# A transformer layer on one core: one engine's order kept in W_down, mixer weights stored by half, transposes in another PSUM bank

## The chip, the cores and the metric

The kernel runs on 1 core of one Trainium2 chip. The metric is the time of one execution on the device in microseconds (us), and the median of 3 runs counts. TensorE (PE) does the matrix products, VectorE (DVE), ScalarE (ACT) and GpSimd (POOL) the rest; SyncE (SP) issues most transfers.

## The reference

One decoder layer over 1024 tokens of width 1024, in float32:

```
h = RMSNorm_pre(x);  P = h @ W_in            # split into u, v, z, xbc, dt
A = u * (causal W_s v + b)                   # gated mixing in chunks of 128, 8 heads
B = Mamba-2 SSD(conv(xbc), dt) * silu(z)     # chunked scan, gated group norm
x = x + RMSNorm_post(concat[A, B] @ W_out)
f = relu(RMSNorm_pre2(x) @ W_up)^2           # 1024 -> 4096
x = x + RMSNorm_post2(f @ W_down)            # 4096 -> 1024
```

## The kernel before, in words

Every float32 product is made of three matmuls. An operand is split into a high part (a cast by ACT into a format that PE takes at full speed) and a low part (the operand less its high part, by DVE or POOL); `mm3` multiplies high by high, high by low and low by high. Names ending in `h` are high parts, those in `l` low ones; `wh` and `wl` are those of a mixer weight unit of 128 x 1024.

The mixer works on two halves of 512 tokens, H0 and then H1. Each half runs over units of `W_in`: the convolved blocks (`psB`, `psC`, `psx`), the state-space groups, then z, v and u (`psu`), then the output projection in units of `W_out` (`pso`). Between them stand a group norm (`psgr` out of `rr`) and the spatial mixing (`pssp`). `units` lists the weight units in the order of use; 28 of them are used by both halves. At first use `load_unit` loads the raw unit into `ws` (2 buffers), splits it, and `keep` stores both parts into DRAM (`wd`); at second use `again` loads both parts. While H0's u is made, `x1_tile` normalizes the four token tiles of the second half and transposes them on PE (`tx`) into `hT`; while H1's u is made, `h2_tile` transposes the MLP's input (`tf`) in the same way. A transposition fills two PSUM banks a tile; ACT takes the high part out (`hTh`), then DVE the low part (`hTl`). PSUM has 4 general banks (`mm_bank`), 2 for the state space (`ss_bank`) and 2 more (`mi_bank`); `psu` and `pso` lie in general ones.

W_up and W_down use a Strassen scheme with seven products for eight. In W_down `seq` lists pieces in super groups; the numbers 1, 5, 6, 3, 7, 2, 4 are the order of the products in one. A piece is 24 matmuls out of `f` (activations read back from DRAM, split by ACT and POOL) and `whd`, `wld` (a weight block `wr`, or a difference of blocks `wt` that DVE makes, split by ACT and DVE). The loop issues `preps[m + 2]` and then the matmuls of piece m; when a product is complete, `flush` adds its PSUM bank `pd` to an accumulator (`acc`): ACT copies the first time, DVE adds later. Two `pd` banks take turns, so PE can begin a new product only when the bank's last one has been flushed. A last group of plain products (`pl`) and the final norm follow.

The order of each engine's instructions is set by a scheduler that plays the program on a simulated timeline, except where `Engine.held` is true: each instruction of that engine is then tied behind the one that the program issued before it. Before, that holds in W_up for PE (`pe.held`), and at the tail for DVE. All instructions issued through `Engine` carry line 73 in the profile, so that they are told apart by their names.

Of the kernel before, what the change touches and what calls it, by code (L numbers as in the profile page):

```python
# [8 lines left out]
F32 = mybir.dt.float32  # L9
F32R = mybir.dt.float32r  # L10
# [5 lines left out]
P = 128  # L16
SEQ = 1024
D = 1024
# [16 lines left out]
N_SPLIT = 5  # L35
# [21 lines left out]
def hymba_kernel(ctx, tc, x, norm_mix_pre, w_in, gm_ln_w, gm_ln_b, gm_w_s, gm_b_s,  # L57
                 conv_w, conv_b, dt_bias, a_log, d_skip, ssm_norm_w, w_out,
                 norm_mix_post, norm_ffn_pre, w_up, w_down, norm_ffn_post, out):
    nc = tc.nc  # L60
# [21 lines left out]
    pe, act, dve, pool = [Engine(e) for e in (nc.tensor, nc.scalar, nc.vector, nc.gpsimd)]  # L82

    def pool_of(stack, name, **k):
        return stack.enter_context(tc.tile_pool(name=name, bufs=1, reuse_waits="tile", **k))
# [5 lines left out]
    wpool = pool_of(ctx, "wpool")  # L91
# [9 lines left out]
    dram = ctx.enter_context(tc.tile_pool(name="dram", bufs=1, space=bass.MemoryType.DRAM))  # L101
# [10 lines left out]
    def f(ap):  # L112
        return ap.bitcast(F32)
# [5 lines left out]
    def split_psum(h, l, src):  # L119
        act.copy(h, src)  # L120
        dve.tensor_tensor(l, src, f(h), op=ALU.subtract)
# [14 lines left out]
    def rstd_steps(ss, n, base=None):  # L136
        nsmall[0] += 1
        i = nsmall[0]
        w = ss.shape[-1]
        v = const.tile([P, w], F32, tag=f"rv{w}", bufs=2 if w == 1 else 1, name=f"rv{i}")  # L140
        r = const.tile([P, w], F32, tag=f"rr{w}", bufs=4 if w == 1 else 1, name=f"rr{i}")
        t = const.tile([P, w], F32, tag=f"rt{w}", bufs=2 if w == 1 else 1, name=f"rt{i}")
        ti = const.tile([P, w], I32, tag=f"rti{w}", bufs=2 if w == 1 else 1, name=f"rti{i}")
        yield r
        if base is None:
            dve.tensor_scalar(v, ss, 0.5 / n, 0.5 * EPS, op0=ALU.mult, op1=ALU.add)
        else:
            dve.tensor_scalar(v, ss, 0.5 / n, base, op0=ALU.mult, op1=ALU.add)
        yield
        dve.tensor_scalar(ti, v.bitcast(I32), 1, None, op0=ALU.logical_shift_right)  # L150
        yield
        dve.tensor_scalar(r.bitcast(I32), ti, -1.0, RSQRT_SEED, op0=ALU.mult, op1=ALU.add)
        for _ in range(3):
            yield
            if w == 1:
                dve.tensor_scalar(t, r, r, v, op0=ALU.mult, op1=ALU.mult)
            else:
                dve.tensor_mul(t, v, r)
                dve.tensor_mul(t, t, r)
            yield  # L160
            if w == 1:
                dve.tensor_scalar(r, t, 1.5, r, op0=ALU.subtract, op1=ALU.mult)
            else:
                dve.scalar_tensor_tensor(r, t, 1.5, r, op0=ALU.subtract, op1=ALU.mult)

    def row_rstd(ss, n, base=None):
        steps = rstd_steps(ss, n, base)
        r = next(steps)
        for _ in steps:
            pass  # L170
        return r
# [24 lines left out]
    units = xbu + zvu + wou[0:4] + xbu[0:4] + wou[4:8] + xbu[4:8] + zvu + wou  # L196
# [3 lines left out]
    ready = []  # L200
    loads = []
# [5 lines left out]
    staged = {}  # L207

    def stage_unit(i):
        kind, src = units[i]  # L210
        shape = [P, 8, P] if kind == "m" else [P, 2, 512]
        st = stage.tile(shape, F32, tag="ws", bufs=N_STAGE, name=f"ws{i}")
        loads.append(nc.sync.dma_start(st, src).ins.name)
        staged[i] = st, shape

    first, parts = {}, {}

    def load_unit(eng=None):
        i = state["load"]
        if i >= len(units):  # L220
            return
        state["load"] += 1
        if id(units[i]) in first:
            again(i)
            return
        first[id(units[i])] = i
        if i not in staged:
            stage_unit(i)
        st, shape = staged.pop(i)
        wh = wpool.tile(shape, F32R, tag="wh", bufs=N_SPLIT, name=f"wh{i}")  # L230
        wl = wpool.tile(shape, F32R, tag="wl", bufs=N_SPLIT, name=f"wl{i}")
        split(wh, wl, st, eng)
        ready.append((wh, wl))
        keep(i)

    def keep(i):

        if any(u is units[i] for u in units[i + 1:]):
            parts[i] = [dram.tile([P, 1024], F32, name=f"wd{i}{j}") for j in range(2)]
            for d, t_ in zip(parts[i], ready[i]):  # L240
                nc.sync.dma_start(d, f(t_.rearrange("p a b -> p (a b)")))

    def again(i):
        shape = [P, 8, P] if units[i][0] == "m" else [P, 2, 512]
        hl = [wpool.tile(shape, F32R, tag=t_, bufs=N_SPLIT, name=f"{t_}{i}") for t_ in ("wh", "wl")]
        for d, t_ in zip(parts[first[id(units[i])]], hl):
            ins = nc.sync.dma_start(f(t_.rearrange("p a b -> p (a b)")), d)
        loads.append(ins.ins.name)
        ready.append(tuple(hl))

    def next_unit(ahead=2, eng=None):
        i = state["use"]
# [6 lines left out]
    def norm_w(src, name, unit=None):  # L259
        w = now["nwp"].tile([P, D], F32, tag="nw", bufs=2, name=name)  # L260
        d = nc.sync.dma_start(w, src[0].partition_broadcast(P))
        if unit is not None:
            after(d, unit)
        return w

    def load_tok(src, name, unit=None):
        t = now["tok"].tile([P, D], F32, tag="tok", bufs=4, name=name)
        d = nc.sync.dma_start(t, src)
        if unit is not None:
            after(d, unit)  # L270
        return t

    x0 = {}
    for what in PRO_LOADS:
        if what == "w":
            wpre = norm_w(norm_mix_pre, "wpre")
        elif what in "ab":
            stage_unit("ab".index(what))
        else:
            t = int(what)  # L280
# [14 lines left out]
    def sumsq(src, name, ss=None):  # L295
        if ss is None:
            ss = const.tile([P, 1], F32, tag="ss", bufs=8, name=name)
        junk = now["tok"].tile([P, src.shape[-1]], BF16, tag="junk", bufs=1, name=f"{name}j")
        act.activation(junk, src, AF.Square, accum_out=ss)
        return ss  # L300

    def norm_transpose(xx, r, w, hT, t, name, bank):
        dve.scalar_tensor_tensor(xx, xx, r, w, op0=ALU.mult, op1=ALU.mult)
        transpose_split(xx, hT, t, name, bank)

    def transpose_split(xx, hT, t, name, bank):
        for q in range(2):
            ps = bank(f"{name}_{q}")
            pv = ps.rearrange("p (k c) -> p k c", c=P)
            for k in range(4):  # L310
                pe.transpose(pv[:, k, :], xx[:, (4 * q + k) * P:(4 * q + k + 1) * P], ident)
            split_psum(hT[0][:, 4 * q:4 * q + 4, t * P:(t + 1) * P],
                       hT[1][:, 4 * q:4 * q + 4, t * P:(t + 1) * P], pv)

    hT_tag = "hTh", "hTl"
    hT = tuple(hpool.tile([P, KB, HALF], F32R, tag=t_, bufs=1, name=t_) for t_ in hT_tag)

    def x1_tile(t):
        xx = load_tok(x[0, HALF + t * P:HALF + (t + 1) * P, :], f"x1_{t}", X1_AFTER + t)
        norm_transpose(xx, row_rstd(sumsq(xx, f"ssx1{t}"), D), wpre, hT, t, f"tx1{t}", mm_bank)  # L320

    mctx = stack()
    mpool = pool_of(mctx, "mpool")
# [477 lines left out]
    H0.v = tok_dense_gelu(H0, "v", dense_tok)  # L801
    v_norm(H0)
    H0.u = tok_dense_gelu(H0, "u", dense_tok_outer, lambda t: t and x1_tile(t - 1))
    x1_tile(3)
    wpost = norm_w(norm_mix_post, "wpost", X1_AFTER)
    wfpre = norm_w(norm_ffn_pre, "wfpre", X1_AFTER)
# [33 lines left out]

    def h2_tile(t):
        xx = load_tok(h2d[t * P:(t + 1) * P, :], f"h2r{t}")
        transpose_split(xx, hT, t, f"tf{t}", mm_bank)

    H1.u = tok_dense_gelu(H1, "u", dense_tok_outer, lambda t: t and h2_tile(t - 1))
    h2_tile(3)
    spatial(H1)
    sctx.close()
# [229 lines left out]
    for p in range(N_PAIR):  # L1078
        ahead = prep(p + 1)
        a = A[p]  # L1080
# [61 lines left out]
    def rows(g, h):  # L1142
        n, gi = sg_of[g]
        return raw_tile(2 * n + h)[:, 4 * gi:4 * gi + 4, :].rearrange("p (r c) n -> p r c n", r=2)

    def w_load(n, h, gs=None):
        for g in gs or SG[n]:
            for r in range(2):
                d = nc.sync.dma_start(rows(g, h)[:, r], downs[4 * g + 2 * r + h][1])
                wr_loads.append(d.ins.name)  # L1150
# [63 lines left out]
    def flush(i, ps):  # L1214
# [3 lines left out]
        else:  # L1218
            act.copy(a_, ps)
            done.add(INTO[i])  # L1220

    w_load(0, 0)
    floads[0]()
    w_load(0, 1)
# [147 lines left out]
```

## Time and profile before

| | us |
|---|---|
| median of 3 runs (1070.23 to 1070.66) | 1070.66 |
| profiled execution | 1074.9 |
| its span | 1073.1 |
| PE busy in it | 1023.7 |
| DVE, ACT, POOL busy | 743.8, 468.6, 313.3 |
| mean granted TensorE clock | 0.984 of full speed |

The stages, in us from the span's start: H0's mixer to about 172, H0's output projection and H1's mixer to 427, W_up to 741, W_down to 1020, the plain group to 1061, the last norm to the end. A busy share says little of a single stage; waits and windows do. In a timeline the bracket tells how long the engine was idle just before and on which instruction it waited.

### The profile page before, as it was taken

What the parts mean: (1) busy time and instruction counts of PE and PEld (TensorE: products, weight loads), DVE (VectorE), ACT (ScalarE), POOL (GpSimd) and SP (SyncE); (2) the same over time, 40 slices, a digit from 0 to 9 for tenths busy, and PEclk for the clock granted to TensorE, in tenths of its full rate; (3) what the DMA queues carried; (4) which work ended last, traced back from release to release, by engine and by line L of the source; (5) the groups of instructions that cost most, each with busy time, mean ns of one, the idle gap of its engine ahead of it and who ended that gap; (6) DMA issues with size and microseconds to landing.
All of it is one profiled execution on the core that took longest, in us unless ns stands there. A gap on an engine that the chain in (4) does not pass through costs nothing. (4 is left out here: it accounts for less than half of the span.)

```text
span 1073.1 us, 13234 instructions
## 1 busy us (share of the span) xinstructions
PE 1023.7 (95%) x4735; PEld 836.4 (78%) x4735; DVE 743.8 (69%) x1265; ACT 468.6 (44%) x642; POOL 313.3 (29%) x169
## 2 busy tenths in 40 slices
PE   5989998999999999999999999999699999999996
PEld 4777776777788888888788888787588888888885
DVE  5647978366954835677477777775976777776677
ACT  5547443244343423675444444445533333333421
POOL 4454332030001002400111111112734444444533
PEclk9999898999999999999999999999989999999998
DMA  8997745475974263766756677766842552443422
GB/s 267 313 320 279 259 172 196 137 247 185 389 269 165 97 223 121 229 195 200 249 194 219 230 235 235 228 215 238 309 157 98 177 177 84 145 152 136 145 84 98
DMA packets 138857, 216.46 MB, mean 202 GB/s; under 512 B 9652, under 2 KB 72232, under 8 KB 138792
## 3 DMA queue, kind: packets, MB, share of 16 engines
q1 hardware_dynamic: 104360, 196.74, 53.1%
q10 hardware_dynamic: 34432, 18.88, 6.0%
q8 instruction: 37, 0.61, 0.2%
q14 instruction: 28, 0.23, 0.1%
HBM read 143.73 MB, written 71.86 MB: 201 GB/s over the span
## 5 line engine op out<-in xcount | busy, mean ns | idle before, releaser
L73 PE MATMUL pd<-whd,f 128*128 128x512 f32 x752 | 234.2, 392 | 7.9 <-DVE acc L73 7.9
L73 PEld LDWEIGHTS pd<-whd,f 128*128 128x128 f32 x752 | 142.3, 189 | 38.2 <-DVE acc L73 8.4
L73 POOL TENSOR_TENSOR f<-fr,f 128x1024 fp32r<-128x1024 f32 x47 | 118.5, 2524 | 147.2 <-ACT f L73 147.2
L73 PE MATMUL pd<-wld,f 128*128 128x512 f32 x376 | 147.4, 392 | 0.8 <-DVE wld L73 0.8
L73 POOL TENSOR_TENSOR wl<-ws,wh 128x1024 fp32r<-128x1024 f32 x36 | 87.7, 2440 | 191.9 <-ACT wh L73 191.7
L73 ACT CAST f<-fr 128x1024 fp32r<-128x1024 f32 x47 | 49.4, 1053 | 146.2 <-issue 132.2
L73 POOL TENSOR_TENSOR wlb<-sa,whb 128x1024 fp32r<-128x1024 f32 x16 | 38.5, 2407 | 225.1 <-ACT whb L73 213.9
L73 PEld LDWEIGHTS pd<-wld,f 128*128 128x128 f32 x376 | 71.3, 190 | 16.1 <-DVE wld L73 1.2
L73 DVE TENSOR_TENSOR wld<-wt,whd 128x1024 fp32r<-128x1024 f32 x28 | 63.5, 2267 | 26.9 <-ACT whd L73 26.9
L73 ACT ACTIVATE u<-u 128x512 f32<-128x512 f32 (+1 forms) x66 | 44.3, 672 | 61.6 <-DVE u L73 55.7
L73 ACT CAST wh<-ws 128x1024 fp32r<-128x1024 f32 x44 | 46.1, 1049 | 53.1 <-DMA ws<-in_w_in_dram 17.5
L73 DVE TENSOR_TENSOR acc<-pd,acc 128x2048 f32<-128x2048 f32 x24 | 54.9, 2287 | 14.8 <-PE pd L73 14.8
L73 DVE TENSOR_TENSOR wld<-wr,whd 128x1024 fp32r<-128x1024 f32 x21 | 47.8, 2276 | 22.8 <-ACT whd L73 22.8
L73 ACT ACT_TABLE_LOAD x30 | 38.5, 1283 | 27.9 <-DVE gg L73 8.7
L73 PE MATMUL pe<-hTh,wh 128*128 128x512 f32 x128 | 50.3, 393 | 0.0
L73 PE MATMUL pe<-hTh,wl 128*128 128x512 f32 x128 | 49.9, 390 | 0.0
L73 PE MATMUL pe<-hTl,wh 128*128 128x512 f32 x128 | 49.9, 390 | 0.0
L73 DVE TENSOR_TENSOR u<-puB,s 128x512 f32<-128x512 f32 x32 | 22.1, 692 | 31.6 <-DMA s<-early 15.8
L73 DVE TENSOR_SCALAR gg<-gg,acs 128x128 f32<-128x128 f32 x64 | 21.4, 396 | 19.9 <-DMA gg<-acd 19.9
L73 PE MATMUL pso<-wh,mixbh 128*128 128x512 f32 x64 | 28.0, 438 | 6.6 <-DVE hTl L73 5.3
L73 DVE TENSOR_TENSOR wlc<-sa,whc 128x1024 fp32r<-128x1024 f32 x16 | 29.2, 1824 | 5.6 <-ACT whc L73 5.6
L73 ACT CAST whd<-wt 128x1024 fp32r<-128x1024 f32 x28 | 29.3, 1046 | 5.7 <-DVE wt L73 2.8
(342 smaller groups left out, 2652.2 us busy)
## 6 DMA issues: line engine op xcount, KB each, us to landing
fr<-fsp SPq DMA_DIRECT2D x49, 512.0 KB, 3.8
wu<-in_w_up_dram ACTq DMA_DIRECT2D x32, 512.0 KB, 5.1
wr<-in_w_down_dram SPq DMA_DIRECT2D x32, 512.0 KB, 5.5
wd<-wh SPq DMA_DIRECT2D x28, 512.0 KB, 4.0
wd<-wl SPq DMA_DIRECT2D x28, 512.0 KB, 5.2
wh<-wd SPq DMA_DIRECT2D x28, 512.0 KB, 4.6
wl<-wd SPq DMA_DIRECT2D x28, 512.0 KB, 4.2
fsp<-c SPq DMA_DIRECT2D x42, 256.0 KB, 2.1
```

The costliest lines, as they stand in the source:

```text
L73: ins = fn(*a, **k)
```

## The change

Three edits. First, `dve.held = True` stands before W_down's loop and no longer only before the tail, so that DVE works in the order in which the loop issues: low parts and differences for piece m + 2, then the flush of piece m. Second, `keep` stores only `wl`; `again` loads the raw weight once more from the input into a `ws` buffer, makes `wh` with an ACT cast, and loads `wl` from DRAM. Third, `x1_tile` and `h2_tile` transpose into the two `ss_bank` banks and not into the general ones.

```diff
@@ keep, again
         if any(u is units[i] for u in units[i + 1:]):
-            parts[i] = [dram.tile([P, 1024], F32, name=f"wd{i}{j}") for j in range(2)]
-            for d, t_ in zip(parts[i], ready[i]):
-                nc.sync.dma_start(d, f(t_.rearrange("p a b -> p (a b)")))
+            parts[i] = dram.tile([P, 1024], F32, name=f"wd{i}")
+            nc.sync.dma_start(parts[i], f(ready[i][1].rearrange("p a b -> p (a b)")))
 
     def again(i):
-        shape = [P, 8, P] if units[i][0] == "m" else [P, 2, 512]
-        hl = [wpool.tile(shape, F32R, tag=t_, bufs=N_SPLIT, name=f"{t_}{i}") for t_ in ("wh", "wl")]
-        for d, t_ in zip(parts[first[id(units[i])]], hl):
-            ins = nc.sync.dma_start(f(t_.rearrange("p a b -> p (a b)")), d)
-        loads.append(ins.ins.name)
-        ready.append(tuple(hl))
+        if i not in staged:
+            stage_unit(i)
+        st, shape = staged.pop(i)
+        wh, wl = [wpool.tile(shape, F32R, tag=t_, bufs=N_SPLIT, name=f"{t_}{i}") for t_ in ("wh", "wl")]
+        nc.sync.dma_start(f(wl.rearrange("p a b -> p (a b)")), parts[first[id(units[i])]])
+        act.copy(wh, st)
+        ready.append((wh, wl))
@@ x1_tile
-        norm_transpose(xx, row_rstd(sumsq(xx, f"ssx1{t}"), D), wpre, hT, t, f"tx1{t}", mm_bank)
+        norm_transpose(xx, row_rstd(sumsq(xx, f"ssx1{t}"), D), wpre, hT, t, f"tx1{t}", ss_bank)
@@ h2_tile
-        transpose_split(xx, hT, t, f"tf{t}", mm_bank)
+        transpose_split(xx, hT, t, f"tf{t}", ss_bank)
@@ before W_down's loop
+    dve.held = True
     w_load(0, 0)
```

The scheduler makes new orders of these. On DVE at W_down's start, before: the number in `wld_3` or `pd_5` is that of the product (product 3 goes on in the bank of product 5, `acc_6525` is the accumulator that it is added to), and the last number tells instances apart.

```order
L73 TENSOR_TENSOR wld_3_6608<-wr_6533,whd_3_6607 128x1024
L73 TENSOR_TENSOR wt_0_6566<-wr_6533,wt_0_6566 128x1024
L73 TENSOR_TENSOR wld_7_6644<-wt_0_6645,whd_7_6643 128x1024
L73 TENSOR_TENSOR wt_2_6866<-wr_6596 128x1024
L73 TENSOR_TENSOR wld_2_6681<-wr_6533,whd_2_6680 128x1024
L73 TENSOR_TENSOR wld_4_6716<-wt_0_6566,whd_4_6715 128x1024
L73 TENSOR_TENSOR wt_1_6908<-wr_6781,wt_1_6829 128x1024
L73 TENSOR_TENSOR wld_1_6752<-wr_6596,whd_1_6751 128x1024
L73 TENSOR_TENSOR wt_2_6945<-wr_6781,wt_2_6866 128x1024
L73 TENSOR_TENSOR acc_6525<-pd_5_6611,acc_6525 128x2048
```

The same place in the change:

```order
L73 TENSOR_TENSOR wld_3_6608<-wr_6533,whd_3_6607 128x1024
L73 TENSOR_TENSOR wt_0_6645<-wr_6533,wr_6528 128x1024
L73 TENSOR_TENSOR wld_7_6644<-wt_0_6645,whd_7_6643 128x1024
L73 TENSOR_TENSOR wld_2_6681<-wr_6533,whd_2_6680 128x1024
L73 TENSOR_TENSOR acc_6525<-pd_5_6611,acc_6525 128x2048
L73 TENSOR_TENSOR wt_0_6566<-wr_6533,wt_0_6566 128x1024
L73 TENSOR_TENSOR wld_4_6716<-wt_0_6566,whd_4_6715 128x1024
L73 TENSOR_TENSOR acc_6527<-pd_1_6570,acc_6527 128x2048
```

The first DVE `acc` moved up: it now stands right behind the low part for product 2, and the instructions for product 4 and for the next super group come after it.

On PE, at the end of H0's last `psu`, before: `tx` are the transposes of the second half's tiles 2 and 3, `pso_00` the first bank of the output projection.

```order
L73 MATMUL psu_1663<-wh_1511,hTl 128x512
L73 MATMUL tx_0_1708<-ident,x_2_1689 128x128 x4
L73 MATMUL tx_1_1715<-ident,x_2_1689 128x128 x4
L73 MATMUL tx_0_1742<-ident,x_3_1723 128x128 x4
L73 MATMUL tx_1_1749<-ident,x_3_1723 128x128 x4
L73 MATMUL pso_00_1816<-wh_1822,mixbh_1225 128x512
L73 MATMUL pso_00_1816<-wl_1823,mixbh_1225 128x512
```

In the change:

```order
L73 MATMUL psu_1623<-wh_1473,hTl 128x512
L73 MATMUL pso_00_1776<-wh_1782,mixbh_1197 128x512
L73 MATMUL pso_00_1776<-wl_1783,mixbh_1197 128x512
L73 MATMUL pso_00_1776<-wh_1782,mixbl_1198 128x512
L73 MATMUL pso_00_1776<-wh_1782,mixbh_1197 128x512
L73 MATMUL pso_00_1776<-wl_1783,mixbh_1197 128x512
L73 MATMUL pso_00_1776<-wh_1782,mixbl_1198 128x512
L73 MATMUL pso_01_1777<-wh_1782,mixbh_1197 128x512
L73 MATMUL pso_01_1777<-wl_1783,mixbh_1197 128x512
L73 MATMUL tx_0_1668<-ident,x_2_1649 128x128 x4
```

The output projection moved ahead of the transposes; those of tile 3 now stand behind `psgr`.

On PE at the program's start, before: `psB` and `psC` are the first two convolved blocks of H0.

```order
L73 MATMUL psB_0_296<-hTh,wh_148 128x256
L73 MATMUL psC_0_430<-hTh,wh_232 128x256
L73 MATMUL psC_0_430<-hTl,wh_232 128x256
L73 MATMUL psB_0_296<-hTl,wh_148 128x256
L73 MATMUL psB_0_296<-hTh,wl_149 128x256
```

In the change:

```order
L73 MATMUL psB_0_290<-hTh,wh_148 128x256
L73 MATMUL psC_0_422<-hTh,wh_230 128x256
L73 MATMUL psC_0_422<-hTl,wh_230 128x256
L73 MATMUL psx_0_486<-hTh,wh_284 128x256
L73 MATMUL psx_0_486<-hTl,wh_284 128x256
L73 MATMUL psB_0_290<-hTl,wh_148 128x256
L73 MATMUL psB_0_290<-hTh,wl_149 128x256
```

Two matmuls of the third block, `psx`, moved up among those of the first two.

## Rows read from the trace of the kernel before

**Rows 1.** The page's busy times by engine, with share and instructions.

```profile
PE 1023.7 (95%) x4735; PEld 836.4 (78%) x4735; DVE 743.8 (69%) x1265; ACT 468.6 (44%) x642; POOL 313.3 (29%) x169
```

**Rows 2.** Windows (PE, PEld, DVE, ACT, POOL busy; clock; DMA share; GB/s), full stretches.

```profile
300.00:400.00 100.00, 100.00 (x513) 82.70 (x512) 55.99 (x140) 35.53 (x49) 8.10 (x9) 1.00 0.50 177
...
500.00:600.00 100.00, 99.42 (x435) 81.09 (x434) 63.34 (x87) 46.71 (x66) 16.86 (x7) 1.00 0.68 222
...
800.00:900.00 100.00, 100.00 (x443) 82.84 (x442) 76.21 (x39) 36.09 (x36) 43.77 (x19) 1.00 0.42 139
```

**Rows 3.** Waits of PE (total us, times, longest us).

```profile
PE pd L73 <- DVE acc L73: 7.9, 1, 7.9
PE pso L73 <- DVE hTl L73: 5.3, 2, 4.0
PE psC L73 <- DVE gg L73: 3.3, 1, 3.3
...
PE psgr L73 <- DVE rr L73: 2.7, 1, 2.7
```

**Rows 4.** Windows around the two largest waits.

```profile
170.00:180.00 10.00, 6.05 (x34) 5.00 (x33) 10.00 (x11) 6.33 (x8) 7.08 (x3) 0.96 0.89 308
180.00:190.00 10.00, 8.69 (x33) 6.60 (x31) 4.11 (x13) 0.00 (x0) 0.73 (x1) 0.69 0.66 236
...
775.00:780.00 5.00, 2.15 (x5) 1.76 (x6) 5.00 (x4) 0.00 (x0) 2.81 (x1) 0.50 0.51 150
780.00:785.00 5.00, 5.00 (x16) 3.92 (x16) 3.49 (x3) 0.00 (x0) 0.00 (x0) 0.65 0.18 64
```

**Rows 5.** Timeline of DVE at W_down's start (start us, us, instruction).

```profile
758.83 1.21 DVE L73 TENSOR_TENSOR wld<-wt,whd 128x1024 fp32r<-128x1024 f32 x1
...
762.23 3.42 DVE L73 TENSOR_TENSOR wld<-wt,whd 128x1024 fp32r<-128x1024 f32 x1
...
775.52 2.28 DVE L73 TENSOR_TENSOR acc<-pd,acc 128x2048 f32<-128x2048 f32 x1
```

**Rows 6.** Timeline of POOL in the same stretch.

```profile
761.07 16.74 POOL L73 TENSOR_TENSOR f<-fr,f 128x1024 fp32r<-128x1024 f32 x5 [4.39 <-ACT f L73]
```

**Rows 7.** DVE's groups in W_down, 800 to 900 (busy us, mean ns, idle before).

```profile
L73 DVE TENSOR_TENSOR wld<-wt,whd 128x1024 fp32r<-128x1024 f32 x11 | 26.5, 2406 | 9.2 <-ACT whd L73 9.2
...
L73 DVE TENSOR_TENSOR wld<-wr,whd 128x1024 fp32r<-128x1024 f32 x8 | 18.6, 2325 | 11.4 <-ACT whd L73 11.4
```

**Rows 8.** Timeline of PE at H0's output projection.

```profile
172.81 1.91 PE L73 MATMUL tx<-ident,x 128*128 128x128 f32 x16
178.66 0.50 PE L73 MATMUL pso<-wh,mixbh 128*128 128x512 f32 x1 [3.95 <-DVE hTl L73]
...
182.39 0.80 PE L73 MATMUL pso<-wh,mixbh 128*128 128x512 f32 x1 [1.31 <-DVE hTl L73]
...
188.37 1.05 PE L73 MATMUL psgr<-ident,rr 128*128 128x128 f32 x8
```

**Rows 9.** Timeline of DVE there.

```profile
177.93 0.68 DVE L73 TENSOR_TENSOR hTl<-tx,hTh 128x512 fp32r<-128x512 f32 x1
...
183.59 0.15 DVE L73 SCALAR_TENSOR_TENSOR rr<-rt,rr 128x4 f32<-128x4 f32 x1
```

**Rows 10.** Timeline of ACT at the program's start.

```profile
22.22 1.05 ACT L73 CAST wh<-ws 128x1024 fp32r<-128x1024 f32 x1 [4.75 <-DMA ws<-in_w_in_dram]
```

**Rows 11.** Timeline of PE at the program's start.

```profile
19.67 0.28 PE L73 MATMUL psB<-hTh,wl 128*128 128x256 f32 x1
19.79 0.28 PE L73 MATMUL psB<-hTh,wh 128*128 128x256 f32 x1
...
24.38 1.86 PE L73 MATMUL tx<-ident,x 128*128 128x128 f32 x15 [1.21 <-ACT x L73]
```

**Rows 12.** DMA issues: packets' size, median us to landing.

```profile
wh<-wd SPq DMA_DIRECT2D x28, 512.0 KB, 4.6
...
ws<-in_w_in_dram SPq DMA_DIRECT2D x20, 512.0 KB, 6.6
```

## Prediction

> **What bounds the kernel now.** I read the page's busy shares first. TensorE (PE) works 1023.7 us of a span of 1073.1 us and no other engine more than 743.8 [rows 1], so time can be gained only where PE stands idle or runs at its lower clock, some 49 us in all, and it is lost wherever an edit makes PE wait. Windows along the span come next: the reader should see that PE is full between 300 and 400, almost full in W_up between 500 and 600, and full in W_down's middle between 800 and 900 [rows 2]. So a change of ours must be judged in the remaining stretches. The waits of PE name them [rows 3]: 7.9 us once in W_down, for VectorE (DVE) to add a finished PSUM bank to an accumulator (`acc`), 5.3 us in two waits for DVE's `hTl` at the start of the first half's output projection, 3.3 us for `gg` and 2.7 us for `rr` in the mixer. The clock in windows comes last: after the two largest waits the granted TensorE clock is 0.69, 0.50 and 0.65 of full speed [rows 4], so that part of the time PE is at the lower of its two levels, 1.2 GHz. A wait is thus dearer than its idle time. The order of each engine's program, of before and of the change, says what stands ahead of the waited-for instructions.
>
> All sums stand against the profiled execution, which took 1074.9 us (span 1073.1); the median of the runs is 1070.66, 4.2 us less, and I take the change to be the same in both.
>
> **Edit 1, W_down's DVE order: -9 us.** In 100 us of steady W_down PE runs 443 matmuls [rows 2], 0.226 us each; a piece of 24 is 5.4 us. PE resumes when `acc` ends, at 775.52 + 2.28 = 777.8 [rows 5]; it stood 7.9 us, so it ran dry at 769.9. The bank had been complete one piece earlier, at about 764.5. DVE took `acc` only at 775.5 because the scheduler had put subtractions for later pieces ahead of it: from 762.23 on four instructions of 3.4 us each, 13.3 us in all [rows 5]. They are so long because POOL makes five `f` pieces in that time [rows 6]; the same kind of instruction took 1.21 us at 758.83. In the changed order these four come behind `acc`, and ahead of it stands only what the pieces up to number 2 need. DVE had done all that by 762.2. Should the order now serialize those a little later, one more subtraction of 3.4 us fits between 764.5 and 769.9 together with the 2.3 us of `acc`. So the 7.9 us go. The clock goes with them: from 775 to 785 PE ran 5 + 16 matmuls [rows 4]; the 7.2 us after 777.8 would hold 32 at 0.226 us, so 11 are missing, 2.5 us. Together 10.4.
>
> What is late next: piece 4, behind it. Its difference and its low part now come after `acc`: 766.8 + 3.4 + a ScalarE (ACT) cast of 1.05 + 3.4 = 774.7, and PE wants them at 769.9 + 5.4 = 775.3. This is close, but a miss costs little, as the following `acc` and weights have a whole piece each. I take 9; the ends are 10.4 and, if one of the 3.4 us instructions falls in the way twice, 3.
>
> In the steady part the program order puts the ACT cast between a difference and its low part, so that DVE waits in order. In 800 to 900 DVE works 76.2 us [rows 2]; 11 of the 19 pieces there have a difference [rows 7], and if each of these waits a whole cast, 11 x 1.05 = 11.6 us are added: 87.8 of 100. PE would not notice. I take 0.
>
> **Edit 3, transposes of x's second half and of h2 in the state-space banks: -4.5 us.** Before, the last 16 transposes (`tx`) start at 172.81 and last 1.9 us; they hold the general banks, and the first `pso` matmul starts at 178.66 after 3.95 us of idle time, the seventh at 182.39 after 1.31 us [rows 8]: both wait for DVE's `hTl`, which empties those banks, at 177.93 [rows 9]. The unit of 24 `pso` matmuls lasts from 178.66 to 188.37, 9.7 us with a wait of 1.3 inside, where 5.4 are needed: 3.0 us went to the clock (0.69 in that window [rows 4]). In the change the `pso` banks depend only on ACT's copies of `psu`, and the order puts `pso` right behind `psu`, with `tx` in between. PE would be through with the transposes of tile 2 and the unit at about 172.8 + 5.4 + 1.0 + 0.6 = 180. But what follows, `psgr`, needs `rr`, whose last step before began at 183.59 [rows 9] on a DVE that was never idle from 170 to 180 [rows 4]. So `rr` is late next: 188.37 - 183.8 = 4.6 us are gained, up to 8.3 if DVE gets to `rr` sooner, and near 0 if the two-bank transposes make DVE later still. I take 4.5. For h2 the same edit has no idle time to remove: PE is full there [rows 2]. With two banks instead of four those transposes may wait for DVE, but the order has whole units of matmuls around them; 0, with 1 us against us.
>
> **Edit 2, only the low part in DRAM: +2 us.** 28 stores go (the `wh` half; 28 units are read back [rows 12]) and each repeated unit gets an ACT cast, 1.05 us [rows 10], in all 29.4 us. The re-reads move the same bytes, but the raw `w_in` blocks land in 6.6 us instead of 4.6 [rows 12]. Are the casts hidden? W_up is the nearest stretch: it loads, casts and subtracts every unit in just this way, and PE is idle 0.6 us of 100 there [rows 2]. Bounds: 0 if all are hidden, 29.4 if none. I take the end that the W_up row is near to, +0.5, for ACT's order in the second half's first blocks, where a cast now stands between evacuations.
>
> At the program's start the order changes too: two `psx` matmuls come after only 15 of the first block's, at about 19.5, and their weight was cast at 22.22 to 23.27 [rows 10, 11]. Before, PE had other work until 23.2, and the transposes that it needed anyway began at 24.38 and ended at about 26 [rows 11]. Now it waits up to 3.8 us and has that work still to do: 22 matmuls at 0.12 and transposes of 1.6 end at about 27.7, so 1.7 us are lost; with a load that comes an us earlier, as one store fewer stands ahead of it, less. I take +1.5, between 0 and 4 (with the clock). In the first half's middle the waits for `gg` and `rr` [rows 3] may shrink, as SyncE no longer waits to store `wh`, or grow, as other matmuls were moved behind them: 0, within 2 either way.
>
> The sum: -9 - 4.5 + 0.5 + 1.5 = -11.5 us: 1063.4 for the profiled execution, **1059 us** for the median.
>
> **A rule weighed.** POOL's five `f` take 16.74 us beside DVE instructions of 3.4 us, which alone take 1.21 [rows 5, 6]. The Trainium skill (page "SBUF — State Buffer", section "Who interferes with whom") says that VectorE and GpSimd share a pair of SBUF ports under an exclusive lock. The trace agrees with it. It speaks against edit 1: a DVE that stops for a cast hands the port to POOL each time, which is the third rival.
>
> **The rivals.**
> First, the wait in W_down mostly changes place: piece 4 or the first weight of the next group is late by what `acc` gained, since DVE and POOL still block each other. For it: the margin of 0.6 us worked out above. Against: only one or two pieces are tight. Gain there 3 instead of 9: 1065. Chance 0.17.
> Second, `rr` or the transposes themselves hold the output projection: edit 3 gives 0 to 1, as DVE was busy all the time from 170 to 180 [rows 4]. 1063. Chance 0.12.
> Third, slower: in steady W_down every low part finds POOL on the port and takes 3.4 us instead of 2.4 [rows 5, 7]. 19 a 100 us make 19 us more, 76.2 + 11.6 + 19 = 106.8 of 100: 7 us lost per 100, and 19 in the 270 us of W_down, against 11.5 gained: 1078. It decides from (100 - 87.8) / 19 = 0.64 us per low part on. Against it: the low parts before waited for casts too (20.6 us of DVE's idle time [rows 7]) and still took 2.4. Chance 0.05. The casts in ACT's queue would end on the same side from 11.5 / 28 = 0.4 us of exposure each; chance 0.03.
> Fourth, more: `gg` and `rr` come early enough as well, and their waits and the clock behind them, some 6 us, go with the start unharmed: 1052. Chance 0.10.
> Fifth, gains eaten by the start and by the second half: within 0.2%. Chance 0.03.
>
> **How the numbers follow.** The forecast's own case, 1055 to 1063, has 0.50. The range of 1051 to 1067 takes in the first, second and most of the fourth rival, and leaves out the rest, some 0.2 with the edges. Two runs of this kernel can be told apart from about 0.2%, 2.1 us. Faster than 1068.5: 0.50 + 0.17 + 0.12 + 0.10 = 0.89; the same: 0.03; slower: 0.05 + 0.03 = 0.08.
>
> **What would show it.** In W_down PE has no wait of more than 2 us and `acc` of the fourth piece runs before 768; the clock stays at 1.00 from 770 to 785. At the output projection the first `pso` follows `psu` at once, and a wait of PE names `rr`. The waits list shows `psx` or `psC` on ACT's `wh` near 20. No PE wait between 250 and 700 names ACT's `wh` for more than 1 us. The prediction is wrong if a wait on `wld` recurs in W_down, if PE's idle time in the mixer grows by more than 4 us, or if `pso` still waits for `hTl`.

## The result and the profile after

The changed kernel takes 1055.44 us (median of 4 runs, 1053.31 to 1057.69) against 1070.49 for the kernel before: the ratio is 0.986, 95% interval 0.9836 to 0.9884. It is 15 us faster; 1059 was forecast. The profiled execution took 1057.69 us, its span 1055.9 us against 1073.1 before.

The page's busy times, to be read beside [rows 1]:

```profile
PE 1017.1 (96%) x4735; PEld 829.8 (79%) x4735; DVE 753.3 (71%) x1265; ACT 494.5 (47%) x670; POOL 316.6 (30%) x169
```

VectorE (DVE) is busier by 9.5 us, ScalarE (ACT) by 25.9, and TensorE (PE) works 6.6 us less at the same matmuls: that much clock came back.

To see where the time went I cut the profiled spans where PE starts the first half's last `psu` matmul, the second half's first `psd`, the first `pe`, the first `pd` and the first `pl`. Lengths in us, with the experiments told of below (each is one profiled execution, and stages that an edit doesn't touch differ by 1 to 2, W_up by up to 4):

```
kernel (edits)         to psu      to psd  to pe  to pd  to pl  to end
before                    172.6     37.3   217.5  313.8  278.7   53.2
changed (1, 2, 3)         169.3     30.0   219.8  314.8  267.9   54.1
e1 (1)                    174.1     38.1   218.9  312.0  267.8   54.3
e2 (2)                    167.4     36.1   219.3  311.7  277.7   52.9
e3 (3, x1 alone)          170.9     33.2   218.8  313.6  278.6   53.1
e4 (3, h2 alone)          174.8     37.2   217.8  316.0  277.6   53.1
e5 (1, 3)                 170.5     33.2   217.9  311.8  267.9   54.2
e6 (2, 3)                 168.6     30.1   220.1  311.9  280.6   52.9
e7 (2, stores kept)       172.8     38.6   218.6  311.7  280.6   53.1
e8 (1 in part, 2, 3)      170.5     30.1   220.0  311.9  271.7   52.9
e12 (1, 2, 3 without h2)  169.6     30.1   219.5  312.2  267.9   54.6
```

W_down ("to pl") is 10.8 us shorter, the output projection ("to psd") 7.3 and the first half's mixer 3.3; the second half is 2.3 longer, W_up 1.0 and the end 0.9. Together -17.2, the difference of the spans; 2 us of it are the two profiled executions' distance from their medians (4.4 and 2.3 above).

The waits of PE (total, times, longest), to be read beside [rows 3]:

```profile
...
PE tx L73 <- DVE x L73: 2.7, 1, 2.7
PE psB L73 <- POOL xde L73: 2.5, 3, 1.8
...
PE psx L73 <- ACT wh L73: 1.5, 1, 1.5
...
PE pso L73 <- ACT mixbh L73: 1.3, 1, 1.3
...
PE psC L73 <- DVE gg L73: 0.9, 1, 0.9
...
PE pd L73 <- DVE wld L73: 0.8, 1, 0.8
PE pl L73 <- DVE acc L73: 0.8, 1, 0.8
```

The wait for `acc` in W_down and those of `pso` for `hTl` are gone, and so is that of `psgr` for `rr`, which stood in the first half's middle (at 128.69) and not at the output projection; `gg` costs 0.9 and not 3.3. What came instead is small, the largest after the program's start 2.5 in three pieces, for POOL's `xde`. The windows of the same stretches (columns as in [rows 2] and [rows 4]):

```profile
170.00:180.00 10.00, 9.75 (x55) 7.88 (x53) 8.45 (x19) 4.94 (x6) 4.57 (x2) 1.00 0.98 322
180.00:190.00 10.00, 8.44 (x41) 6.89 (x41) 4.14 (x9) 5.15 (x8) 2.58 (x2) 1.00 0.77 246
230.00:240.00 10.00, 7.69 (x28) 5.71 (x27) 3.88 (x13) 6.66 (x10) 0.61 (x1) 0.83 0.70 213
775.00:780.00 5.00, 5.00 (x24) 4.14 (x23) 4.57 (x2) 3.08 (x4) 2.50 (x1) 1.00 0.09 21
780.00:785.00 5.00, 5.00 (x24) 4.14 (x23) 1.79 (x2) 2.55 (x3) 2.49 (x1) 1.00 0.25 97
800.00:900.00 100.00, 100.00 (x443) 82.81 (x442) 86.02 (x39) 37.09 (x37) 46.31 (x20) 1.00 0.46 156
```

From 170 to 190 and from 775 to 785 the clock is at 1.00 where it was 0.69, 0.50 and 0.65 [rows 4]. From 230 to 240 it is 0.83: there PE waits 1.0 and 1.3 us for ACT's `xg` and `cd` in the second half, as it did before without losing clock. DVE in 800 to 900 works 86.0 us, not 76.2 [rows 2].

In the first half the gain is mostly clock. From the first `psbt` (at 48 us) to the last `psu` PE runs the same matmuls. Before, with two windows out of that stretch:

```profile
48.24:172.58 124.34, 116.61 (x582) 94.00 (x581) 93.81 (x237) 65.37 (x89) 48.72 (x32) 0.96 0.69 242
80.00:100.00 20.00, 20.00 (x99) 15.84 (x98) 13.52 (x35) 15.05 (x18) 9.56 (x7) 0.91 0.76 267
120.00:140.00 20.00, 17.32 (x81) 13.50 (x80) 18.97 (x47) 5.00 (x7) 9.19 (x9) 0.83 0.75 250
```

After:

```profile
48.42:169.31 120.89, 113.95 (x582) 89.97 (x580) 89.97 (x234) 64.59 (x88) 47.17 (x31) 1.00 0.51 166
```

PE's idle time there is 6.9 us and was 7.7, but in pieces of up to 1.8 us and not 3.3; its busy time is 2.7 us shorter, since the clock no longer falls behind the waits for `gg` and `rr`.

W_down's start on DVE, and POOL beside it, to be read beside [rows 5, 6]:

```profile
757.11 2.29 DVE L73 TENSOR_TENSOR acc<-pd,acc 128x2048 f32<-128x2048 f32 x1 [3.11 <-ACT f L73]
759.32 2.77 DVE L73 TENSOR_TENSOR wt<-wr,wt 128x1024 f32<-128x1024 f32 x1
```

```profile
753.53 10.82 POOL L73 TENSOR_TENSOR f<-fr,f 128x1024 fp32r<-128x1024 f32 x4 [5.28 <-ACT f L73]
```

The first `acc` runs 23.2 us after the first `pd` matmul (733.94); before it ran 34.3 after (741.24). Behind it stands a difference of 2.8 us, and POOL's `f` pieces still share the time. The output projection on PE, the last step of `rr` on DVE, and the program's start on ACT and PE, beside [rows 8 to 11]:

```profile
172.31 0.60 PE L73 MATMUL tx<-ident,x 128*128 128x128 f32 x4
...
176.01 1.05 PE L73 MATMUL psgr<-ident,rr 128*128 128x128 f32 x8
```

```profile
175.11 0.16 DVE L73 SCALAR_TENSOR_TENSOR rr<-rt,rr 128x4 f32<-128x4 f32 x1
```

```profile
19.93 1.04 ACT L73 CAST wh<-ws 128x1024 fp32r<-128x1024 f32 x1 [2.63 <-DMA ws<-in_w_in_dram]
```

```profile
21.03 0.39 PE L73 MATMUL psx<-hTh,wh 128*128 128x256 f32 x1 [1.47 <-ACT wh L73]
...
24.01 1.91 PE L73 MATMUL tx<-ident,x 128*128 128x128 f32 x16
```

The unit of `pso` matmuls now runs from 169.5 on with `tx` in between, and `psgr` follows at 176.01 without a wait, since `rr` was done at 175.3. At the start `psx` waits 1.5 us for a weight that was cast at 19.93, 2.3 us earlier than before.

### The profile page after: what moved, and what is told of

Same layout as the page of the kernel before. It is cut to its first block, busy times and chain, and to the rows that moved or that the text cites. A ratio compares the mean times of both kernels' runs of the same rounds, so it can differ in the third digit from the quotient of the medians.

```text
span 1055.9 us, 13174 instructions
## 1 busy us (share of the span) xinstructions
PE 1017.1 (96%) x4735; PEld 829.8 (79%) x4735; DVE 753.3 (71%) x1265; ACT 494.5 (47%) x670; POOL 316.6 (30%) x169
## 4 chain that ended last, share of the span: by engine, by line
PE 74%; DVE 10%; DMA 8%; ACT 3%; issue 2%; SPq 2%; POOL 1%; DVEq 0%; ACTq 0%; POOLq 0%
PE pd L73 25%; PE pso L73 8%; PE pe L73 6%; PE puB L73 5%; PE puC L73 5%; PE psu L73 4%; PE pl L73 4%; PE psz L73 3%; PE puD L73 3%; PE psB L73 2%; PE psv L73 2%; DMA wu<-in_w_up_dram 2%; PE psC L73 2%; DMA gg<-acd 2%; PE psx L73 1%
## 5 line engine op out<-in xcount | busy, mean ns | idle before, releaser
L73 ACT CAST wh<-ws 128x1024 fp32r<-128x1024 f32 x72 | 75.3, 1046 | 73.4 <-DMA ws<-in_w_in_dram 13.8
L73 ACT CAST whd<-wt 128x1024 fp32r<-128x1024 f32 x28 | 29.4, 1052 | 93.9 <-DVE wt L73 93.4
L73 DVE TENSOR_TENSOR wld<-wt,whd 128x1024 fp32r<-128x1024 f32 x28 | 36.7, 1309 | 35.2 <-ACT whd L73 34.0
L73 DVE TENSOR_TENSOR wld<-wr,whd 128x1024 fp32r<-128x1024 f32 x21 | 57.8, 2783 | 0.5 <-ACT whd L73 0.5
L73 DVE TENSOR_TENSOR wt<-wr,wt 128x1024 f32<-128x1024 f32 x14 | 35.9, 2562 | 0.0
L73 ACT ACTIVATE f<-f 128x512 f32<-128x512 f32 x32 | 20.2, 632 | 27.3 <-DVE f L73 26.8
```

The costliest lines, as they stand in the source:

```text
L73: ins = fn(*a, **k)
```

## Experiments

Each is measured against the kernel before, run beside it on the same chip; experiments and the changed kernel are compared with each other by these ratios.

**e1, edit 1 alone.**

```diff
+    dve.held = True
     w_load(0, 0)
```

> Only edit 1 (VectorE keeps the program's order in W_down); everything up to W_down is as before. Theory: the wait of TensorE for the first acc and the low clock behind it go, and nothing comes in their place: 10 to 11 us less, 1060, with no wait of TensorE over 2 us between 720 and 1000. Rival: what the change gained in W_down needed other data or timings that edits 2 and 3 bring there; then half of it or less, 1065 or more. Second rival: the serial order costs VectorE so much that the last pieces are late: slower than 1066.

Measured: 1062.13, ratio 0.9924 (0.9902 to 0.9947), 8 us less, 2 short of the theory. W_down is 267.8 us, as in the changed kernel, and PE's only waits there are 0.8 for `wld` and 0.8 for the `acc` ahead of `pl`. The end is 1.1 us longer: that wait for `acc` is new, and the last two low parts now stand behind this flush. The edit needs nothing of the others.

**e2, edit 2 alone** (the hunks of `keep` and `again`).

> Only edit 2 (only the low part stored, the high part made again by ScalarE). Theory: the first half's middle gains some 3 us (the waits for gg and rr shrink since SyncE no longer waits for ScalarE's casts to store them), the start and the second half's casts cost 1 to 3, in sum 0 to 3 us less: 1068 to 1071. Rival: the casts in ScalarE's queue are what made the second half 2.3 us longer, and the start costs as forecast: 2 to 4 us more, 1073 to 1075. Second rival: the middle's gain belongs to edit 2 alone and nothing is paid: 1066.

Measured: 1068.32, ratio 0.9983 (0.9966 to 0.9999). By the stages the first half's mixer gains 5 us and the second half loses 2. The theory held in the sum; the first half's gain is larger than it had it.

**e3, edit 3 for x's second half alone.**

```diff
-        ... f"tx1{t}", mm_bank)
+        ... f"tx1{t}", ss_bank)
```

> Only the transposes of x's second half go into the state-space banks. Theory: the waits of the output projection for hTl and the low clock behind them go: 5 to 8 us less, 1063 to 1066. Rival: rr, the next thing that it needs, is as late as before unless edit 2 relieves VectorE and SyncE: 2 to 4 us less, 1067 to 1069, with a wait of TensorE for rr near 180.

Measured: 1067.09, ratio 0.9963 (0.9942 to 0.9984). The output projection is 33.2 us and not 37.3. PE there, and its first `psgr`; then DVE and POOL:

```profile
128.78 0.49 PE L73 MATMUL psgr<-ident,rr 128*128 128x128 f32 x2 [2.85 <-DVE rr L73]
...
179.65 1.33 PE L73 MATMUL tx<-ident,x 128*128 128x128 f32 x8 [1.90 <-DVE hTl L73]
180.81 1.67 PE L73 MATMUL psgr<-ident,rr 128*128 128x128 f32 x8
```

```profile
176.71 2.29 DVE L73 SCALAR_TENSOR_TENSOR rr<-rt,rr 128x4 f32<-128x4 f32 x1
...
180.37 0.16 DVE L73 SCALAR_TENSOR_TENSOR rr<-rt,rr 128x4 f32<-128x4 f32 x1
```

```profile
176.61 2.37 POOL L73 TENSOR_TENSOR wl<-ws,wh 128x1024 fp32r<-128x1024 f32 x1 [2.82 <-ACT wh L73]
```

The rival's time came out, and its mechanism in part. `pso` no longer waits for `hTl`, but the transposes themselves do, 1.9 us in the two banks. The rival's sign, a wait for `rr` near 180, is not there: the run's wait of 2.9 for `rr` is that of the first half's middle, as before:

```profile
128.69 0.80 PE L73 MATMUL psgr<-ident,rr 128*128 128x128 f32 x2 [2.68 <-DVE rr L73]
```

`rr` is close behind all the same: it was done at 180.5, and without the transposes' wait `psgr` could have started at 178.9 (an estimate, 180.81 - 1.90), so that it would have waited for `rr` then. One step of it took 2.29 us where the others take 0.16; it began 0.1 us behind a low part on POOL and ended with it.

**e4, edit 3 for h2 alone** (the same in `h2_tile`).

> Only the transposes of h2 go into the state-space banks. Theory: TensorE had no idle time there, so nothing to gain: within 1 us of before, 1070 to 1071. Rival: two banks for four tiles make TensorE wait for VectorE to empty them, which is the second half's loss of 2.3 us: 1072 to 1073, with a wait of TensorE's tf or of what follows it between 340 and 400.

Measured: 1070.18, ratio 0.9998 (0.9975 to 1.0021). No wait of `tf` or `pso` between 340 and 400. Worth nothing.

**e5, edits 1 and 3.**

> Edits 1 and 3 without edit 2 (both parts stored and read back, as before). Edits 1 and 3 alone gave ratios of 0.9924 and 0.9963. Theory: their places are apart, so they add: 0.989, some 1059. The rest to the changed kernel, 3 to 4 us, is edit 2's: the first half's middle (to the last psu) is as long as before, 171 to 174 us, and the output projection from the last psu to the second half's start takes 33 us as with edit 3 alone, not 30. Rival: edit 2 only helps the output projection that edit 3 has opened (rr is earlier): then the first part is no longer here than in the changed kernel, about 169.

Measured: 1057.47, ratio 0.987 (0.9848 to 0.9893), and the product of e1 and e3 (0.989) lies within. The stages behave as the theory has it: 170.5 and 33.2, and the transposes wait 2.4 for `hTl` there. But the changed kernel's 0.986 is within this interval: against e5 edit 2 gains 1.2 us in the first half and 3.2 in the output projection, loses 1.9 in the second half, and W_up differs by 3.0, within its scatter. About 1 us is left by the ratios, which these runs can't tell from nothing; e12, the same but for a part worth nothing, would make it 4.

**e6, edits 2 and 3.**

> Edits 2 and 3 without edit 1: W_down ordered by the scheduler again. Theory: the wait for the first acc and the low clock come back, W_down takes 278 to 279 us, not 268, and the tail is a microsecond shorter: 1064 to 1066. Rival: other arrival times at W_down's start change the scheduler's order there, so that a part of the wait stays away: 1058 to 1061.

Measured: 1066.94, ratio 0.9956 (0.994 to 0.9971). Waits of PE:

```profile
PE pd L73 <- DVE acc L73: 9.3, 1, 9.3
...
PE psgr L73 <- DVE rr L73: 1.3, 1, 1.3
```

The wait for `acc` is back, with 9.3 us, and W_down takes 280.6. The wait for `rr` is at the output projection (176.81). The theory held, a microsecond or two beyond its upper edge.

**e7, edit 2 with the high parts stored all the same.**

```diff
+            both = dram.tile([P, 1024], F32, name=f"we{i}")
+            nc.sync.dma_start(both, f(ready[i][0].rearrange("p a b -> p (a b)")))
             parts[i] = dram.tile([P, 1024], F32, name=f"wd{i}")
```

> Edit 2 alone, but the 28 high parts are still stored, to places that nobody reads. Theory: the first half's gain in edit 2 (to the last psu 167 us, before 173 to 175) comes from the stores that are gone, which stood in SyncE's queue ahead of the loads and of gg until ScalarE had cast: here it is lost, 172 or more, the wait for gg is 3 us or more again, and the time is 1072 to 1074, as the casts are still paid. Rival: the gain comes from the scheduler's new order of TensorE and VectorE alone, whatever it is made of, and the stores cost nothing: as edit 2 alone, 1068.

Measured: 1077.01, ratio 1.0041 (1.0022 to 1.0059), slower than before and, by the ratios, 6 us slower than e2. Waits of PE:

```profile
PE pso L73 <- DVE hTl L73: 4.7, 2, 4.0
PE psC L73 <- DVE gg L73: 4.4, 1, 4.4
```

The waits are those of the kernel before [rows 3], and the first half takes 172.8 again, where e2 takes 167.4. The 28 stores are thus what edit 2 saves in the first half; the rest of it costs 4 us net. Part of this is the scheduler, which orders the engines anew: W_down, in which none of these stores stands, is 2.9 us longer than in e2. How the stores delay `gg` is seen on SyncE's queue and in the time that `acd` takes from issue to landing (the last number, in us). Before:

```profile
64.11 0.48 SPq L550 DMA_DIRECT2D acd<-acsT  x1
...
68.98 0.32 SPq L241 DMA_DIRECT2D wd<-wh  x1
69.42 1.29 SPq L606 DMA_DIRECT2D gg<-acd  x2
```

After the change:

```profile
62.46 0.94 SPq L550 DMA_DIRECT2D acd<-acsT  x1
66.54 0.81 SPq L606 DMA_DIRECT2D gg<-acd  x2
```

The landing of `acd`, first before, then after the change, then in e7:

```profile
acd<-acsT SPq DMA_DIRECT2D x1, 16.0 KB, 5.2
```

```profile
acd<-acsT SPq DMA_DIRECT2D x1, 16.0 KB, 4.1
```

```profile
acd<-acsT SPq DMA_DIRECT2D x1, 16.0 KB, 6.0
```

`acd` is a copy in DRAM of the state space's decays (`acsT`), and `gg` reads it back, spread over all partitions; so it can't go before that has landed, at 69.3 before and at 66.5 now. Both times it went at once, so the store of `wh`, which had waited for ACT's cast until 68.98, held `gg` itself up by 0.1 us at most. DVE began on `gg` at 73.84 and now begins at 70.13. Of these 3.7 us `acsT` being ready earlier (61.45, not 62.10) makes 0.65, SyncE's queue ahead of `acd` 1.0, the faster landing of `acd` 1.1 and that of `gg` 0.8, while the DMA engines are busy 0.53 of the time from 60 to 80 us and not 0.97 (0.93 in e7). So by these rows the stores delay `gg` through their places in the queue and, it seems, their traffic; the two were not tried apart.

**e8, edit 1 held for seven pieces only.**

```diff
         if g == gs[-1]:
             flush(i, ps)
+        if m == 6:
+            dve.held = False
```

> The changed kernel, but VectorE's order is held only over the first seven pieces of W_down and again in the tail; between them the scheduler orders it. Theory: the whole gain of edit 1 is at the first flushes, and the held order costs 1 us at the start of the plain group (its last low parts stand behind the last flush): 1 us less than the changed kernel, 1053 to 1055, and VectorE is busy 76 us in 100 in the steady part, not 84 to 86. Rival: the scheduler puts the low parts of the second group ahead of the first flushes as soon as it may, and a part of the wait comes back: 1058 to 1064.

Measured: 1059.88, ratio 0.9887 (0.9866 to 0.9908). Its wait of PE:

```profile
PE pd L73 <- DVE acc L73: 3.2, 3, 1.8
```

The rival was right: with the order released, three later flushes are late by 3.2 us in all, and W_down takes 271.7. The end is 1.2 us shorter, as expected. By these lengths 7 of the 10.8 us belong to the first flush and 3.8 to the next ones. DVE is busy 76.2 us from 800 to 900, as the theory had it. The kernel takes some 3 us more than the changed one, though the two intervals overlap.

**e9 and e10, more work on DVE in W_down.**

```diff
         split(h, l, w_block(g, W_KEY[i]), dve)
+        sub(dve, l[:, 0, :], w_block(g, W_KEY[i])[:, 0, :], f(h)[:, 0, :])   # e9
+        sub(dve, l, w_block(g, W_KEY[i]), f(h))                              # e10
```

> The changed kernel, where VectorE computes the first half of each low part in W_down twice (a 128x512 subtraction more per piece, 0.7 us alone). In the changed kernel VectorE works 86 and 84 us of 100 in steady W_down at 18.4 pieces in 100 us, so 14 to 16 us, 0.8 us a piece, are left. Theory: the margin is real, W_down grows by less than 5 us: 1055 to 1060. Rival: the in-order waits for the casts and for the port that POOL uses have already used it up, and any addition shows in full, 49 x 0.7 = 34 us: 1080 to 1090.

Measured: 1085.63, ratio 1.0111 (1.007 to 1.0152), 27 us above the changed kernel by the ratios; W_down is 28.9 us longer. PE's wait in W_down, and the window and DVE's groups in 800 to 900:

```profile
PE pd L73 <- DVE wld L73: 19.6, 16, 3.4
```

```profile
800.00:900.00 100.00, 96.81 (x417) 79.34 (x418) 89.08 (x54) 34.28 (x35) 44.57 (x17) 0.98 0.40 137
```

```profile
L73 DVE TENSOR_TENSOR acc<-pd,acc 128x2048 f32<-128x2048 f32 x9 | 20.5, 2281 | 0.0
...
L73 DVE TENSOR_TENSOR wld<-wt,whd 128x1024 fp32r<-128x1024 f32 x9 | 11.0, 1225 | 10.0 <-ACT whd L73 10.0
```

The rival was right. DVE is busy 89 us and waits 10 for casts: it has no time left, and `acc` no longer waits for PE at all (0.0). In the changed kernel the same groups read:

```profile
L73 DVE TENSOR_TENSOR wld<-wr,whd 128x1024 fp32r<-128x1024 f32 x10 | 31.8, 3221 | 0.0
L73 DVE TENSOR_TENSOR acc<-pd,acc 128x2048 f32<-128x2048 f32 x9 | 20.6, 2287 | 2.8 <-PE pd L73 2.8
L73 DVE TENSOR_TENSOR wld<-wt,whd 128x1024 fp32r<-128x1024 f32 x10 | 12.2, 1225 | 11.2 <-ACT whd L73 11.2
L73 DVE TENSOR_TENSOR wt<-wr,wr 128x1024 f32<-128x1024 f32 x4 | 11.3, 2823 | 0.0
L73 DVE TENSOR_TENSOR wt<-wr,wt 128x1024 f32<-128x1024 f32 x4 | 10.3, 2574 | 0.0
```

There 86.0 us of work and 11.2 of waits for casts leave 2.8, the time in which `acc` waited for PE. That is the whole margin, 0.15 us a piece; the other 11 of the 14 us of idle time that I had counted on are part of the loop. The time lost agrees: of 34 us added in W_down 28.9 show, and 5, some 0.1 a piece, were taken up. Before, all differences took 1.2 us each:

```profile
L73 DVE TENSOR_TENSOR wt<-wr,wt 128x1024 f32<-128x1024 f32 x5 | 6.1, 1225 | 0.2
```

> The same with the whole low part computed twice (a 128x1024 subtraction more per piece, 1.2 us alone and up to 3.4 beside POOL). Theory: past the margin of 0.8 us, VectorE is the bound in steady W_down: at 1.2 us each 18.4 x 1.2 = 22 of the 15 us left, 7 us lost in 100, 19 in W_down; at 2.4 each 29 lost in 100, 78 in W_down: 1075 to 1130, with waits of TensorE's pd for DVE's wld or acc all over W_down. Rival: TensorE stays full because the copies fill VectorE's waits for casts: within 5 us of the changed kernel.

Measured: 1104.34, ratio 1.028 (1.0239 to 1.0322), 45 us above the changed kernel, inside the theory's range, with `wld` and `acc` waited for 32.3 us.

**e11, the stores of the low part on POOL's queue.**

```diff
-            nc.sync.dma_start(parts[i], f(ready[i][1].rearrange("p a b -> p (a b)")))
+            nc.gpsimd.dma_start(parts[i], f(ready[i][1].rearrange("p a b -> p (a b)")))
```

> The changed kernel, with the 28 stores of the low part issued by POOL, which makes most low parts, and not by SyncE. Theory: SyncE waited 131 us on POOL's wl for these stores; without them the loads and gg behind come earlier, but TensorE's waits in the first half that these could shorten (psx 1.5, gg 0.9, some of the 1.8 for xde) are small: 0 to 3 us less, 1052 to 1056. Rival: POOL's issuing delays its own low parts and xde: 2 to 6 us more, 1057 to 1062.

Measured: 1061.94, ratio 0.9888 (0.9861 to 0.9915), 6 us slower than e12, which ran beside it. PE's largest wait after the start:

```profile
PE psA L73 <- ACT xg L73: 4.8, 2, 3.7
```

The rival's time came out, but not by its mechanism: `xde` costs 0.9 and not 2.5, and DVE's and ACT's work is late instead (`xg` 4.8, `rr` 2.9, `gg` 2.0). All of it lies in the first half (176.0 us to the last `psu`, 169.6 in e12). What delayed these was not tried apart.

**e12, the changed kernel without the h2 bank.**

> The changed kernel, with h2's transposes in the general banks again. Theory: as alone (ratio 0.9998) the h2 bank is worth nothing: within 2 us of the changed kernel, 1053 to 1058. Rival: beside edit 2 it pays, since the second output projection then follows the last psu at once as the first does: 3 to 5 us more without it, 1058 to 1061, with a wait of TensorE's pso for hTl near 370.

Measured: 1055.52, ratio 0.9831 (0.9805 to 0.9857), which can't be told from the changed kernel (0.9836 to 0.9884). The h2 part may be left out; no version clearly beats the changed kernel.

## Why the prediction was right, point by point

The direction held, and so did the two larger terms in place and cause; 11.5 us were forecast, 15 measured. By stages of the profile it is -9.9 for W_down and the end (forecast -9), -7.3 for the output projection (-4.5), -1.0 for the rest of the mixer (+2), and +1.0 for W_up, which no edit touches.

*Edit 1, -9.* W_down is 10.8 us shorter and the end 0.9 longer, -9.9 in the profile and -8 by e1's ratio. The wait for `acc` and the clock behind it went together, as worked out, and piece 4 was not late. Two things in the working were wrong. I put the cost at the plain group's start at nothing; it is 0.9 to 1.1. And the steady part was closer to the edge than the sum said: I reckoned 87.8 us of 100, by adding the waits for casts to DVE's busy time. The measured sum is 86.0 + 11.2 = 97.2. The differences and the low parts out of raw blocks now meet POOL on the port (2.6 to 2.8 us a difference, 3.2 a low part out of a raw block, which took 2.3 [rows 7]), while the low parts behind a cast run alone in 1.2, not 2.4. e9 shows that the third rival, a slower W_down, would have begun at 0.15 us more per low part and not at 0.64. It was given 0.05; the traces don't say that it should have been more, but the margin by which it failed was a quarter of mine, and that the low parts behind a cast would get shorter, which left that margin, was not foreseen: in this the forecast was lucky. The rule weighed there, the exclusive lock of the Trainium skill's page "SBUF — State Buffer" (section "Who interferes with whom"), agrees with these rows: the time beside POOL moved from one kind of instruction to another and did not go.

*Edit 3, -4.5.* Alone it gave -4 by its ratio, 4.1 in the output projection. `pso` follows `psu` at once, as said. That `rr` is late next, by a wait that PE's list names, was said and did not come: in e3 and e5 the transposes wait instead, and in the changed kernel neither does. Together with edit 2 the projection gains 7.3, near the upper end of 8.3 that was tied to an earlier `rr`. `rr` was done 9.6 and 10.1 us behind the start of the last `psu` in e3 and e5, 8.1 in e6, and 6.0 in the changed kernel. With edit 2 beside edit 3 its first step runs about a microsecond sooner and no `hTl` stands between its steps. The last 2 us are luck: in e6 and e12 a step of `rr` falls beside a low part on POOL and takes 2.3 to 2.4 us, and `psgr` waits 1.3; in the changed kernel the last step begins at 175.11 and POOL at 175.21. The h2 part was forecast at nothing and is nothing (e4, e12).

*Edit 2, +2.* This term had the wrong sign: -1.8 by e2's ratio (-3.6 to -0.1). The step that was mis-sized is the first half's middle, put at 0 within 2 either way. From the first `psbt` to the last `psu` it took 124.3 us before and takes 120.9, and 119.9 in e2; e7 takes it back (124.7). I had seen the stores of `wh` on SyncE and called them even. What they cost was not only their places in the queue but also slower landings (e7's rows) and the clock that PE lost behind its waits. The start was put at +1.5 and cost 0.2 (48.2 to 48.4 at the first `psbt`): the weight came 2.3 us earlier, not one, and the wait for `x` [rows 11] went, as `psx`'s wait covers it. That is not sure either: in e8 and e12, the same up to there, `psx` waits 2.0, the clock is 0.83 from 20 to 30 and the start costs 1.6, as forecast. The casts in the second half were put at 0.5. It takes 218.6 to 220.1 us in the kernels with edit 2 and 217.5 to 218.9 in those without. Of this 1.7 us is clock: the loss from 230 to 260 is in every profile with edit 2 but e7's, and without edit 2 in those of e1 and e3 alone. Less that clock, the second half is on average 0.7 us longer with edit 2, about the forecast. That PE was never made to wait over 1 us for ACT's `wh` there held.

*The rivals.* The first (a wait that changes place in W_down) did not come: no wait there is over 0.8 us. Only e8, with the order released, has later ones. The second (0 to 1 for edit 3) was wrong by its number, 4 in e3, though the transposes do wait there. The third is told of above. The fourth, `gg` and `rr` early as well and the clock behind their waits back, is what happened on top of the forecast's case; 1052 was its time, and the measured one lies between the two, as new waits in the first half's middle (`xde` 2.5, `carry` 1.8) and the second half's clock took part of it.

## What to carry to other kernels

Where an in-order engine both prepares the next pieces and empties the accumulators of the last, look at which of its queued instructions releases the engine that is the bound, and put that first: four of 3.4 us ahead of one flush cost 8 us of waiting and 2.5 of clock. An engine's idle time is not its margin when it waits on another engine inside its own loop; read the margin from how long it waits for the bound engine (here 2.8 us of 100, with 14 idle), or add a known piece of work and see. Where a store stands ahead of a load on a queue, look first when the load's data are there: here the store's own wait held it up by 0.1 us, while without 28 stores a small transfer that the load needs landed in 4.1 us and not 5.2. And idle time of the bound engine in many short pieces can be cheaper than in a few long ones: in the first half nearly the same sum of it cost no clock any more.

## What the runs showed of the hardware

The same two waits of 1.0 and 1.3 us in the second half left the granted clock at 1.00 in four profiles (before, e4, e5, e7) and took 1.7 us of it in the ten others (0.83 from 230 to 240 in the changed kernel's); so two profiles can differ by this much at the same waits. Subtractions of 128x1024 on DVE took 1.2 us alone and up to 3.4 beside POOL's of the same size, on average 3.2 for the low parts out of raw blocks in the order held. A step of 128x4 pays as much: 0.16 us alone, it took 2.2 to 2.4 us when it began just behind an instruction of 2.4 us on POOL (e3, e5, e6, e12). An `acc` out of PSUM took 2.3 us beside POOL and alone.
